# A gate table filled by scattered adding DMAs, wider units of the up matrices, and 28 down groups ahead of the up groups

## The chip, the core and the metric

The kernel runs on one core of a Trainium2 chip. The metric is the device time of one execution in microseconds (us); three runs of the kernel before took 2607.8 to 2616.74 us, median 2609.46. The engines are named as in the profile: PE is TensorE, DVE is VectorE, ACT is ScalarE, POOL is GpSimd, SP is SyncE. GpSimd issues the indirect DMAs, SyncE and ScalarE the plain ones.

## The reference

Two transformer blocks on 512 tokens of 1024 channels. The first mixes tokens (pooling and a gated delta rule) and then has a product-key expert layer; the second is gated sparse attention. The change is in the expert layer:

- Each token has 8 heads. A head scores its query halves against two tables of 128 keys, keeps the best 16 of each half, adds them in pairs (only 50 of the 256 pairs can be among the best 16), keeps the 16 best pairs, and makes gates by softmax. Pair (i1, i2) names expert 128 x i1 + i2 of 16384.
- The result is the sum over the 128 chosen experts of gate x gelu(down[e] . x) x up[e], with down and up of 16384 x 1024 float32 values.

## The kernel before, in words

Tokens 0 to 127 fetch the rows of their experts: `fetch` issues an indirect DMA on GpSimd that brings one row of 1024 values for each of 128 tokens (512 KB) into a ring buffer, and `row_step` uses it on VectorE (L1155 for the 128 down rows, L1167 for the 128 up rows, which need all down rows first). Tokens 128 to 511 (384 columns) meet all experts on TensorE, in 32 groups of 512 experts:

- `expert_down(g)`: 4 products of 24 matmuls each (8 slices of channels, three float16 terms, `mm3` at L352 to L354) and a Gelu. Groups below `R1` are computed early, and their result is stored in DRAM (`ged`); `load_gelu` brings it back.
- `load_gates(g)` brings the gates of the group's experts for all 384 tokens from the table `gd` in DRAM. `combine(g)` multiplies them with the gelu values (L1110, VectorE) and splits the product in two 16-bit parts (L1112 on ScalarE, L1113 on GpSimd).
- `expert_up(g)`: 8 products (one per 128 output channels) of 12 matmuls, each added to the residual `hT` by VectorE (L1132).

Every weight unit (1 MB, 128 x 2048 float32) goes the same way, in the order of the list `seq`: load on SP's queue into one of 4 `raw` buffers, three units ahead; squares on ScalarE (L299) for a power-of-two scale (a small chain through TensorE and VectorE); a float16 part on ScalarE (L313) and the rest on VectorE (L314), one unit ahead. Up units go to one of 2 `usp` buffers, all others to one of 3 `sp` buffers.

The table of gates is built in the gate stage. `select(tt)`, for 128 tokens, finds the best pairs with top-16 searches and turns places into expert numbers with one-hot comparisons (L1003, L1005, L1007). `gate_chunk` then makes, for 32 tokens, one-hot rows of i1 (times the gate, in two parts) and of i2 (L1048 to L1052), multiplies them on TensorE into the dense table, copies it on ScalarE (L1061) and stores it. `PLAN` is the order of selects, chunks and early down groups. After it the buffers of the gate stage are freed for the loop: down groups 12 to 31 alternate with up groups by the list `events`.

The framework's scheduler orders the instructions of each engine by priority, which follows program order, and by when it expects operands to be ready; each engine then runs its list in order. Row steps are spread by `tick(n)`: a budget starts at -6 and gains 1.6 per quarter of a fresh down group, and 1.2 or 1.0 at each second product of an up group; a row step is emitted for each whole unit. `issue_after` ties a row step behind the last residual update. What the budget has not released is emitted by `rows_done()` in front of the last up groups, which run in two parts of the tokens under the norms of the next block.

Of the kernel before, what the change touches and what calls it, by code (L numbers as in the profile page):

```python
# [20 lines left out]
P = 128  # L21
S = 512
D = 1024
# [5 lines left out]
GSC = 16384.0  # L29
PAIRS = [(a, b) for a in range(16) for b in range(16) if (a + 1) * (b + 1) <= 16]  # L30
NPAIR = len(PAIRS)
PAIR_ROWS = [(0, 1, 16), (1, 1, 8), (2, 1, 5), (3, 1, 4), (4, 1, 3), (5, 3, 2), (8, 8, 1)]
# [27 lines left out]
def shape_constants():  # L60
# [21 lines left out]
    put(c1, C1, "rcount", np.broadcast_to(1.0 / (np.arange(16)[None] + 1.0), (P, 16)))  # L82
    c2 = np.zeros((P, NC2), np.float32)
# [14 lines left out]
    c3 = np.concatenate([np.repeat(np.arange(P), 2), np.repeat(np.arange(NPAIR), 16)])  # L98
# [3 lines left out]
R1 = 12  # L102
TD = 384
RING = 6
AH = ()
PLAN = "D D s0 D D s1 g0 D g1 g2 D g3 D s2 g4 D g5 g6 D g7 D s3 g8 D g9 g10 D g11"
# [5 lines left out]
R2 = 3  # L112
# [4 lines left out]
def tile_model(ctx: ExitStack, tc: tile.TileContext, A, out, dbg=None, stop=None):  # L117
# [43 lines left out]
    # ------------------------------------------------------------------ constants  # L161
# [7 lines left out]
    c3 = cp.tile([P, 2 * P + 16 * NPAIR], F16, name="c3")  # L169
# [42 lines left out]
    # ------------------------------------------------------------------ weight stream  # L212
# [20 lines left out]
    order, fresh = [], list(range(R1, 32))  # L233
    for i in range(R1):
# [4 lines left out]
    for i in range(32):  # L239
        if i == 0:  # L240
            events += [("D", order[1]), ("D", order[2]), ("L", order[0]), ("C", order[0])]
        elif 1 < i + 1 < 32 and order[i + 1] >= R1 and i + 1 > 2:
            events.append(("D", order[i + 1]))
        if i + 2 < 32 and order[i + 2] < R1:
            events.append(("L", order[i + 2]))
        if i + 1 < 32:
            events.append(("C", order[i + 1]))
        events.append(("U", order[i]))
    for e, g in events:
        if e == "D":  # L250
            for u in range(2):
                plan(("d", g, u), A["down"][g * 2 + u], 2048, "split", group=("d", g))
        elif e == "U":
            for u in range(2):
                plan(("u", g, u), A["up"][g * 2 + u], 2048, "split", group=("u", g), usplit=g != order[31])
# [24 lines left out]
    def advance(i, loads=False, split=0):  # L280
# [38 lines left out]
        def ahead(k):  # L319
            key = seq[at[k]]["key"]  # L320
            name = "d1" if key[0] == "d" and (key[1] < R1 or key[1] in order[1:R2]) else key[0]
            p = URGENT.get(name, (0, 0))[k == "split"]
            return tc.high_priority(p) if p else ExitStack()
# [21 lines left out]
    def descale(e, isx, k=1.0):  # L345
        """1 / (scale of the weights * scale of the data), times k"""
# [25 lines left out]
    def norm_cols(nm):  # L372
        """the sums of squares of a token in its own partition, a column for each 128 tokens"""
# [12 lines left out]
    def cols_bcast(r):  # L386
        """the columns laid along the tokens, in every partition"""
# [6 lines left out]
    def weight_bound(wcol, n, nm):  # L394
        """powers of two (s, 1 / s) with s * max |w| below 2 ** 15"""
# [5 lines left out]
    def norm3_scale(wname, nm):  # L401
        """|x * rstd| <= 32: a power of two that brings x * rstd * w into range"""
# [9 lines left out]
    def norm3(nm, sl, ws, each=None, pool=False):  # L412
        """RMS norm of the tokens sl in two float16 parts"""
# [9 lines left out]
    def spread3(rows3, v):  # L423
        """rows 0..7 of v as three bfloat16 parts, 32 partitions apart"""
# [37 lines left out]
    # beta and decay rows, then their column forms  # L462
# [20 lines left out]
    def delta_gen(half, q4, k4, v4_):  # L483
# [3 lines left out]
        for n in range(NCH):  # L487
# [42 lines left out]
            # inverse of I + L, block by block  # L530
# [159 lines left out]
    # pooled branch  # L690
# [50 lines left out]
    # the delta-rule output, normalised and gated between the projections of the gates  # L741
# [71 lines left out]
    # |h2| <= 32 |gscale| + |shift| <= sqrt(2 (1024 gscale^2 + shift^2))  # L813
# [8 lines left out]
    def range_start(nm):  # L822
        """powers of two (s, 1 / s), lowered to the ranges of the products that follow"""
# [5 lines left out]
    def range_for(t, e, s, inv):  # L829
        """|sum x w| <= sqrt(sum x^2) sqrt(sum w^2), two such terms added"""  # L830
# [73 lines left out]
    # ------------------------------------------------------------------ product-key experts  # L904
    # tokens 0..127 fetch the rows of their experts, tokens 128..511 meet all experts on the tensor engine
# [13 lines left out]
    def top16(items):  # L919
        """(values, work copy, best values, their places) of several rows, step by step"""  # L920
# [38 lines left out]
    V.tensor_scalar(wk[:, 0:1], s_w, 2.0 ** -37, None, op0=ALU.mult)  # L959
    V.tensor_scalar(wk[:, 1:2], inv_w, 2.0 ** 23, None, op0=ALU.mult)  # L960
    iota_m = c3[:, 0:2 * P].rearrange("p (m e) -> p m e", e=2)
    iota_c = c3[:, 2 * P:].rearrange("p (c k) -> p c k", k=16)
    selT = s1.tile([P, 4, TD], F16, name="selT")
    i1T, i2T, ghT, glT = (selT[:, i] for i in range(4))
    gd = drp.tile([TD // 32, 2, P, 64, 32], F32, name="gdram")
    ged = drp.tile([R1, P, 4 * TD], F32, name="gedram")
    rowg = px.tile([P, P], F32, name="rowg")
    rowi = px.tile([P, 2, P], I32, name="rowi")
    rowu = px.tile([P, P], F32, name="rowu")

    def select(tt):
        sl = slice((tt - 1) * P, tt * P)
        if tt in AH:
            advance(last[0], split=2)
        idf = slab("idf")[:, 0:256].rearrange("p (f h k) -> p f h k", f=2, h=NH)
        V.tensor_copy(idf, idx[:, tt])
        V.tensor_scalar(idf[:, 0], idf[:, 0], float(P), None, op0=ALU.mult)
        cand = slab("cand")[:, :NH * NPAIR].rearrange("p (h c) -> p h c", h=NH)
        cide = slab("cide")[:, :NH * NPAIR].rearrange("p (h c) -> p h c", h=NH)
        o = 0  # L980
        for a0, na, nb in PAIR_ROWS:
            n = na * nb
            shp = [P, NH, na, nb]
            dst = lambda t: t[:, :, o:o + n].rearrange("p h (a b) -> p h a b", a=na)
            A1 = lambda t: t[:, 0, :, a0:a0 + na, None].to_broadcast(shp)
            B1 = lambda t: t[:, 1, :, None, 0:nb].to_broadcast(shp)
            V.tensor_tensor(dst(cand), A1(val[:, tt]), B1(val[:, tt]), op=ALU.add)
            G.tensor_tensor(dst(cide), A1(idf), B1(idf), op=ALU.add)
            o += n
# [3 lines left out]
        sel = tp[:, 2 * P:3 * P].rearrange("p (h k) -> p h k", h=NH)  # L993
# [3 lines left out]
        p16 = smp.tile([P, NH, 16], F16, tag="p16", name="p16", bufs=1)  # L997
        V.tensor_copy(p16, pos)
        prs = {}
        for h in range(NH + 2):  # L1000
            if h < NH:
                eq = slab("eq", (P, NPAIR, 16), F16)
                V.tensor_tensor(eq, iota_c, p16[:, h, None, :].to_broadcast([P, NPAIR, 16]), op=ALU.is_equal)  # L1003
                prs[h] = s1.tile([P, NPAIR, 16], F32, tag="eqp", name="eqp", bufs=3)
                G.tensor_tensor(prs[h], eq, cide[:, h, :, None].to_broadcast([P, NPAIR, 16]), op=ALU.mult)  # L1005
            if h >= 2:
                V.tensor_reduce(sel[:, h - 2, :], prs[h - 2].rearrange("p c k -> p k c"), AX.X, ALU.add)  # L1007
# [5 lines left out]
        if tt == 0:  # L1013
            V.tensor_tensor(rowg.rearrange("p (h k) -> p h k", h=NH), ex, sm.to_broadcast([P, NH, 16]), op=ALU.mult)
            # place of expert (u, a, p) in the rows of "up": u, p, a
            e0, e1 = rowi[:, 0], rowi[:, 1]
            V.tensor_copy(e0, tp[:, 2 * P:3 * P])
            r = smp.tile([P, 2, P], I32, tag="ei", name="ei", bufs=1)
            V.tensor_scalar(r[:, 0], e0, 127, 1, op0=ALU.bitwise_and, op1=ALU.logical_shift_left)
            V.tensor_scalar(r[:, 1], e0, 7, 1, op0=ALU.logical_shift_right, op1=ALU.bitwise_and)  # L1020
            V.tensor_scalar(e1, e0, -256, None, op0=ALU.bitwise_and)
            V.tensor_tensor(r[:, 0], r[:, 0], r[:, 1], op=ALU.bitwise_or)
            V.tensor_tensor(e1, e1, r[:, 0], op=ALU.bitwise_or)
            return
# [764 lines left out]
```

## Time and profile before

| | us |
|---|---|
| median of three runs | 2609.46 |
| span of the profiled execution (one core, so also its own time) | 2609.8 |
| TensorE busy | 2302.3 (88%) |
| VectorE busy | 2009.6 (77%) |
| ScalarE busy | 1358.3 (52%) |
| GpSimd busy | 892.5 (34%) |

Stages by the first and last instructions of their tiles: queries 678 to 787 us, gate stage 787 to 1174, loop of down and up groups 1174 to 2090, last two up groups and norms to 2137, second block to the end. In a slice row each digit is the busy share of a fortieth of the span in tenths. A line row gives instructions, busy time (overlaps counted once), the mean duration of one and the idle time before it. Matmul durations overlap, so the spacing of their starts tells the pace.

### The profile page before, as it was taken

Reading aid. Unit: us, or ns where it says so; the run is one execution under the profiler, and the core shown is the slowest. Engines: PE = TensorE matmul, PEld = TensorE weight load, DVE = VectorE, ACT = ScalarE, POOL = GpSimd, SP = SyncE. Lnnn points to the kernel's source line nnn. Section 1 sums busy time; section 2 is a strip of 40 time slices with the busy share of each in tenths; the row PEclk is TensorE's granted clock in tenths of the full one; section 3 lists DMA queues with packets and bytes.
Section 4 is the critical chain, followed back from the end, with each engine's and each line's share of the span. In section 5 each row is a group of like instructions: output and inputs, shape, how many; then the busy total and the mean of one; then the engine's idle time right before and its main releaser. Section 6 shows DMA issues by size and latency. Waiting matters only on the chain.

```text
span 2609.8 us, 37370 instructions
## 1 busy us (share of the span) xinstructions
PE 2302.3 (88%) x14242; PEld 1371.0 (53%) x14242; DVE 2009.6 (77%) x4166; ACT 1358.3 (52%) x1831; POOL 892.5 (34%) x618
## 2 busy tenths in 40 slices
PE   6999999999998766777799888898898989999997
PEld 2337896344654444444455555555554566555545
DVE  6877554396799999877898989889898973766555
ACT  6453223574545566554555555555455565454543
POOL 0002444020003645536666756665565520000000
PEclk9999999999999888889999999999999989999999
DMA  4220002343223443458788888888888724100120
GB/s 190 81 81 33 1 1 102 145 163 112 81 78 125 147 168 146 157 198 309 274 309 303 314 303 304 298 309 296 304 297 309 273 82 156 65 17 33 65 97 33
DMA packets 130771, 440.98 MB, mean 169 GB/s; under 512 B 9504, under 2 KB 61088, under 8 KB 100384
## 3 DMA queue, kind: packets, MB, share of 16 engines
q1 hardware_dynamic: 86272, 267.39, 29.1%
q0 software_dynamic: 36864, 134.23, 14.1%
q10 hardware_dynamic: 7456, 36.97, 3.5%
q8 instruction: 112, 1.84, 0.3%
q14 instruction: 67, 0.55, 0.1%
HBM read 401.86 MB, written 36.70 MB: 168 GB/s over the span
## 4 chain that ended last, share of the span: by engine, by line
PE 35%; DVE 31%; DMA 11%; issue 9%; ACT 8%; POOL 5%; SPq 0%; ACTq 0%; DVEq 0%; POOLq 0%
DVE sp L314 6%; DMA raw<-in_down_dram 4%; PE ps_in L352 4%; PE ps_in L354 4%; PE ps_in L353 4%; POOL ring L1147 3%; DMA raw<-in_up_dram 3%; DVE ohH L1052 2%; DVE rjunk L1155 2%; ACT sp L313 2%; DVE hT L1132 2%; DVE ysum L1167 2%; ACT junk L299 2%; PE ps_r L552 2%; PE ps_x L546 2%
## 5 line engine op out<-in xcount | busy, mean ns | idle before, releaser
L299 ACT ACTIVATE junk<-raw 128x2048 bf16<-128x2048 f32 (+1 forms) x202 | 383.1, 1897 | 354.5 <-DMA raw<-in_up_dram 154.7
L314 DVE SCALAR_TENSOR_TENSOR sp<-raw,scw,sp 128x2048 f16<-128x2048 f32 (+2 forms) x140 | 340.5, 2433 | 103.2 <-ACT sp L313 102.8
L352 PE MATMUL ps_u<-cexp,usp 128*128 128x384 f16 (+2 forms) x1024 | 334.9, 329 | 51.2 <-DVE hT L1132 46.9
L354 PE MATMUL ps_d<-xn,sp 128*128 128x384 f16 x1024 | 341.5, 335 | 38.7 <-DVE sp L314 38.7
L354 PEld LDWEIGHTS <-sp 128*128 128x128 f16 (+1 forms) x2320 | 230.7, 99 | 247.4 <-DVE sp L314 47.6
L352 PE MATMUL ps_d<-xn,sp 128*128 128x384 f16 x1024 | 344.2, 336 | 7.1 <-ACT sp L313 5.5
L313 ACT ACTIVATE sp<-raw,scw 128x2048 f16<-128x2048 f32 (+2 forms) x140 | 276.3, 1979 | 134.4 <-DVE scw L207 101.5
L353 PE MATMUL ps_d<-xn,sp 128*128 128x384 f16 x1024 | 343.8, 336 | 0.0
L352 PEld LDWEIGHTS <-sp 128*128 128x128 f16 (+1 forms) x2320 | 230.9, 100 | 212.2 <-issue 29.8
L353 PE MATMUL ps_u<-cexp,usp 128*128 128x384 bf16 (+2 forms) x1024 | 334.6, 328 | 1.7 <-POOL cexp L1113 1.7
L353 PEld LDWEIGHTS <-sp 128*128 128x128 f16 (+1 forms) x2320 | 230.7, 99 | 197.6 <-issue 26.5
L354 PE MATMUL ps_u<-cexp,usp 128*128 128x384 f16 (+2 forms) x1024 | 330.2, 328 | 3.7 <-DVE usp L314 3.7
L352 PE MATMUL ps_in<-xn,sp 128*128 128x512 f16 (+2 forms) x728 | 272.6, 376 | 5.8 <-DVE cv L479 3.3
L354 PE MATMUL ps_in<-xn,sp 128*128 128x512 f16 (+2 forms) x728 | 272.6, 376 | 1.5 <-DVE sp L314 1.5
L353 PE MATMUL ps_in<-xn,sp 128*128 128x512 f16 (+2 forms) x728 | 272.6, 375 | 0.0
L1147 POOL DMA_INDIRECT ring<-in_down_rows_dram,rowi x128 | 192.3, 1502 | 179.8 <-DVE rjunk L1155 109.8
L1147 POOL DMA_INDIRECT ring<-in_up_dram,rowi x128 | 190.9, 1491 | 176.1 <-DVE ysum L1167 125.9
L1113 POOL TENSOR_TENSOR cexp<-cf,cexp 128x384 bf16<-128x384 f32 x128 | 174.5, 1383 | 36.1 <-ACT cexp L1112 34.9
L1167 DVE SCALAR_TENSOR_TENSOR ysum<-ring,rowg,ysum 128x1024 f32<-128x1024 f32 x127 | 172.1, 1355 | 0.2
L1132 DVE SCALAR_TENSOR_TENSOR hT<-ps_u,yd,hT 128x384 f32<-128x384 f32 (+2 forms) x272 | 153.6, 583 | 21.5 <-PE ps_u L354 21.2
L1155 DVE SCALAR_TENSOR_TENSOR rjunk<-ring,xrow 128x1024 f32<-128x1024 f32 x128 | 164.9, 1288 | 3.1 <-DMA ring<-in_down_rows_dram,rowi 3.0
L353 PEld LDWEIGHTS <-usp 128*128 128x128 f16 x1024 | 102.1, 100 | 116.2 <-issue 58.9
(446 smaller groups left out, 4397.1 us busy)
## 6 DMA issues: line engine op xcount, KB each, us to landing
raw<-in_down_dram SPq DMA_DIRECT2D x64, 1024.0 KB, 5.5
raw<-in_up_dram SPq DMA_DIRECT2D x64, 1024.0 KB, 6.5
raw<-in_w_in_dram SPq DMA_DIRECT2D x45, 1024.0 KB, 4.8
gdram<-stg ACTq DMA_DIRECT2D x24, 1024.0 KB, 5.9
gt<-gdram SPq DMA_DIRECT2D x31, 768.0 KB, 9.0
raw<-in_w_ada_dram SPq DMA_DIRECT2D x12, 1024.0 KB, 4.8
gedram<-gelu ACTq DMA_DIRECT2D x12, 768.0 KB, 4.4
gelu<-gedram SPq DMA_DIRECT2D x12, 768.0 KB, 9.6
```

The lines of the kernel that those rows point to most:

```text
L299: act(junk[:, :e["n"]], e["raw"][:, :e["n"]], AF.Square, accum_out=ss[:, j:j + 1])
L313: act(sp[:, 0, :n], e["raw"][:, :n], AF.Copy, scale=e["s"])
L314: rq["lo"] = V.scalar_tensor_tensor(sp[:, 1, :n], e["raw"][:, :n], e["s"], sp[:, 0, :n], op0=ALU.mult, op1=ALU.subtract)
L352: T.matmul(ps, wh, xh, start=start, stop=False)
L353: T.matmul(ps, wh, xl, start=False, stop=False)
L354: T.matmul(ps, wl, xh, start=False, stop=stop)
L546: T.matmul(px[:, R4(r)], lm[:, R4(r)], Rm[:, R4(r)], start=True, stop=True)
L1113: G.tensor_tensor(ct[:, i, 1, :].bitcast(BF16), c, ct[:, i, 0, :], op=ALU.subtract)
L1132: rq["ins"] = V.scalar_tensor_tensor(o, ps[:, :n], yds[g], o, op0=ALU.mult, op1=ALU.add)
L1147: G.indirect_dma_start(out=r, out_offset=None, in_=src, in_offset=bass.IndirectOffsetOnAxis(ap=rowi[:, s // P, s % P:s % P + 1], axis=0))
L1155: V.scalar_tensor_tensor(jk, r, 1.0, xrow, op0=ALU.mult, op1=ALU.mult, accum_out=rowu[:, s:s + 1])
L1167: V.scalar_tensor_tensor(ysum[0], r, g, ysum[0], op0=ALU.mult, op1=ALU.add)
```

## The change

1. The table. `gd` becomes one array with a cell for each expert and token (expert, token; 16384 x 384 float32). 32 DMAs on SP's queue (`clear_gates`) fill it with zeros during the projections. `select` yields the gates (`gate_w`) and the cell numbers (`gate_i`, 384 x expert + token); `scatter(tt, h)` issues 16 indirect DMAs on GpSimd for head h of 128 tokens, each adding 128 values to 128 cells. Each head's DMAs wait for those of the head before it for the same tokens, the first for the clears; every `load_gates` waits for all. Place to number: no one-hot of 50 places, but comparisons with the 16 starts of the rows of pairs (float16, 16 x 16 x 8, VectorE only) and sums by halving. `gate_chunk` is gone.
2. The up matrices. A unit holds 8 expert tiles by 256 output channels instead of 2 tiles by 1024, with a scale of its own. `expert_up(q)` takes a quad of two groups: 8 products of 24 matmuls, so a residual update per 24 matmuls. `combine` takes two groups at once, one instruction of each kind per group, and the subtraction moves from GpSimd to VectorE. The rows that tokens fetch come from the natural layout (`up_rows`).
3. The order. `R1` 12 to 28: 28 down groups run in the gate stage, four in the loop. Ring of rows 6 to 4, `LAG` 4 to 3. The tick constants stay; the tick after an up product now comes after each of the 8 products of a quad.

```diff
-R1 = 12
+R1 = 28
-RING = 6
-PLAN = "D D s0 D D s1 g0 D g1 g2 D g3 D s2 g4 D g5 g6 D g7 D s3 g8 D g9 g10 D g11"
+RING = 4
+GB = 3
+PLAN = "D s1 D s2 D s3 D D D s0"
...
+    def clear_gates(g):
+        cleared.append(nc.sync.dma_start(gd.rearrange("(g p c t) o -> g p c (t o)", g=32, p=P, c=12)[g],
+                                         zero[:, None, :].to_broadcast([P, 12, P])).ins)
...
+        if 8 <= ct < 40:
+            clear_gates(ct - 8)
...
+        over_a(ge, each(p16), first_, ALU.is_ge)
+        over_a(t2, ge, step_, ALU.mult)
+        over_a(t1, ge, di, ALU.mult)
+        sum_a(st, t2)
+        sum_a(i1, t1)
...
+        over_a(ge, each(st), iota_, ALU.is_equal)
+        over_a(t2, ge, ih[:, 1], ALU.mult)
+        sum_a(i2, t2)
...
+    def scatter(tt, h):
+        key, new = f"scatter{tt}", []
+        for s in range(h * 16, h * 16 + 16):
+            i = G.indirect_dma_start(out=gd, out_offset=bass.IndirectOffsetOnAxis(ap=gate_i[tt][:, s:s + 1], axis=0),
+                                     in_=gate_w[tt][:, s:s + 1], in_offset=None, compute_op=ALU.add).ins
+            tc.declare_no_dep(i, group="scatter", keep=heads.get(tt, []), reason="other cells")
+            tc.add_to_no_dep_group("scatter", i)
+            after(i, heads.get(tt, cleared))
+            new.append(i)
+        heads[tt] = new
...
+        i = q.dma_start(gt, gd.rearrange("(g i p t) o -> g p i (t o)", g=32, i=4, p=P)[g]).ins
+        for tt in heads:
+            after(i, heads[tt])
...
+            V.scalar_tensor_tensor(t, gt, ca[:, 0:1], t, op0=ALU.mult, op1=ALU.mult)
+            nc.scalar.copy(ct[:, 0], t)
+            V.tensor_tensor(ct[:, 1].bitcast(BF16), t, ct[:, 0], op=ALU.subtract)
...
-            for i in range(4):
+            for i in range(8):
+                ct = cexp[2 * q + i // 4]
...
-            elif piece is None and dt_ % 2:
-                tick(TK[1] if g >= R1 else TK[2])
+            elif piece is None:
+                tick(TK[1] if 2 * q >= R1 else TK[2])
...
-    LAG = 4
+    LAG = 3
...
-        else:
-            gate_chunk(int(op[1:]))
+            if op != "s0":
+                for h in range(NH):
+                    scatter(int(op[1:]), h)
```

## Rows read from the trace of the kernel before

**Rows 1.** Page, slices of 65 us: TensorE, VectorE, DMA engines.
```profile
PE   6999999999998766777799888898898989999997
...
DVE  6877554396799999877898989889898973766555
...
DMA  4220002343223443458788888888888724100120
```
**Rows 2.** Windows by stage: start:end, length, busy per engine, granted clock, DMA share, GB/s.
```profile
678.00:787.00 109.00, 102.20 (x575) 58.02 (x574) 99.85 (x535) 55.68 (x70) 0.00 (x0) 0.98 0.25 88
787.00:1174.00 387.00, 277.87 (x2033) 178.70 (x2032) 344.58 (x699) 223.26 (x336) 190.29 (x108) 0.86 0.41 158
1203.00:2090.00 887.00, 786.99 (x4728) 457.62 (x4726) 797.71 (x1116) 468.93 (x490) 539.52 (x373) 0.97 0.84 297
2090.00:2137.00 47.00, 41.73 (x423) 36.45 (x424) 38.49 (x85) 27.23 (x47) 12.36 (x11) 0.93 0.20 69
2137.00:2609.00 472.00, 451.16 (x2687) 248.46 (x2685) 272.26 (x822) 236.10 (x449) 7.05 (x12) 0.98 0.19 69
```
**Rows 3.** Lines of VectorE in the gate stage, 787 to 1174 us.
```profile
L1052 DVE TENSOR_TENSOR ohH<-ohA,selT 128x1024 f16<-128x1024 f16 x48 | 93.4, 1946 | 6.1 <-PE ps_g L1057 6.1
L314 DVE SCALAR_TENSOR_TENSOR sp<-raw,scw,sp 128x2048 f16<-128x2048 f32 x24 | 63.8, 2661 | 17.8 <-ACT sp L313 17.8
...
L1048 DVE TENSOR_TENSOR ohA<-c,selT 128x1024 f16<-128x1024 f16 x48 | 37.7, 786 | 1.9 <-ACT selT L1036 1.9
...
L924 DVE FIND_INDEX8 tp<-tp,cand 128x8 uint32<-128x50 f32 x32 | 5.9, 204 | 0.0
...
L922 DVE MAX8 tp<-cand 128x8 f32<-128x50 f32 x32 | 4.0, 197 | 0.3
```
**Rows 4.** Tile ps_u: count, duration ns, first and last start.
```profile
L352 PE MATMUL ps_u<-cexp,usp x1024: 216/326/528, 1203.7 to 2133.2; 128*128 128x384 f16 x160, 128*128 128x256 f16 x6, 128*128 128x128 f16 x5
```
**Rows 5.** Waits in the loop: total us, times, longest.
```profile
ACT junk L299 <- DMA raw<-in_up_dram: 144.4, 47, 8.9
```
**Rows 6.** Timeline of TensorE at the first down group.
```profile
786.99 0.32 PE L353 MATMUL ps_d<-xn,sp 128*128 128x384 f16 x1
787.16 0.33 PE L354 MATMUL ps_d<-xn,sp 128*128 128x384 f16 x1
```
**Rows 7.** Timeline of GpSimd at the first row fetches.
```profile
1177.72 2.93 POOL L1147 DMA_INDIRECT ring<-in_down_rows_dram,rowi  x1 [0.30 <-issue]
1180.95 0.94 POOL L1147 DMA_INDIRECT ring<-in_down_rows_dram,rowi  x1 [0.30 <-issue]
1182.20 0.93 POOL L1147 DMA_INDIRECT ring<-in_down_rows_dram,rowi  x1 [0.31 <-issue]
```
**Rows 8.** Timelines of VectorE and GpSimd around 2050 us.
```profile
2050.41 2.35 DVE L314 SCALAR_TENSOR_TENSOR sp<-raw,scw,sp 128x2048 f16<-128x2048 f32 x1
...
2050.58 3.00 POOL L1147 DMA_INDIRECT ring<-in_up_dram,rowi  x1 [1.81 <-DVE dsc L348]
```
**Rows 9.** Lines of GpSimd and VectorE in the loop, 1203 to 2090 us.
```profile
L1147 POOL DMA_INDIRECT ring<-in_up_dram,rowi x128 | 190.9, 1491 | 176.1 <-DVE ysum L1167 125.9 <-DVE ssb L199 15.4 <-DVE dsc L348 7.4
...
L1167 DVE SCALAR_TENSOR_TENSOR ysum<-ring,rowg,ysum 128x1024 f32<-128x1024 f32 x127 | 172.1, 1355 | 0.2
...
L314 DVE SCALAR_TENSOR_TENSOR usp<-raw,scw,usp 128x2048 f16<-128x2048 f32 x60 | 141.8, 2379 | 5.5 <-ACT usp L313 5.4
L1132 DVE SCALAR_TENSOR_TENSOR hT<-ps_u,yd,hT 128x384 f32<-128x384 f32 x240 | 141.4, 606 | 16.4 <-PE ps_u L354 16.1
L1110 DVE SCALAR_TENSOR_TENSOR cf<-gt,cs,gelu 128x384 f32<-128x384 f32 x124 | 101.0, 831 | 23.9 <-POOL cexp L1113 18.4 <-ACT gelu L1084 5.5
```
**Rows 10.** Tile ring: time from issue to landing.
```profile
DMA to landing us min/median/max: 4.0/7.5/17.4
```
**Rows 11.** DMA in the loop: queues (packets, MB, share of 16 engines); gate loads.
```profile
q1 hardware_dynamic: 61980, 132.56, 43.6%
q0 software_dynamic: 35751, 130.15, 40.4%
...
gt<-gdram SPq DMA_DIRECT2D x30, 768.0 KB, 9.0
```

More of the change, by code (lines that the diff above doesn't have):

```diff
@@ L97, in shape_constants @@
     put(c2, C2, "qs", 0.125 / slopes[np.arange(4)[None] + 4 * (p[:, None] // 64)])
[L98 removed]
+    step = np.append(np.diff([0] + FIRST)[:15], 0)
+    c3 = np.concatenate([np.repeat(v, 8) for v in (np.array(FIRST), step, np.arange(16))])
     return c1, c2, np.broadcast_to(c3[None], (P, c3.size)).astype(np.float16)
[L102 removed]
+R1 = 28
 TD = 384
[L104 to L106 removed]
+RING = 4
+GB = 3
+PLAN = "D s1 D s2 D s3 D D D s0"
 SL3 = 40
@@ L111 @@
 URGENT = {"d1": (0, 0), "d": (50, 50), "u": (50, 50)}
-R2 = 3
 TK = (1.6, 1.2, 1.0)
@@ L232, in tile_model @@
         plan(("q", u), A["w_query"][u], 2048, "split")
-    order, fresh = [], list(range(R1, 32))
-    for i in range(R1):
+    order, fresh = [], list(range(R1 // 2, 16))
+    for i in range(R1 // 2):
         order.append(i)
@@ L238, in tile_model @@
     events = [("D", g) for g in range(R1)]
-    for i in range(32):
+    prep = lambda q: [("D" if g >= R1 else "L", g) for g in (2 * q, 2 * q + 1)]
+    pre = {i: prep(q) for i, q in enumerate(order)}
+    for i in range(16):
         if i == 0:
[L241 to L246, printed above, removed]
+            events += pre[0] + [("C", order[0])] + [e for e in pre[1] if e[0] == "D"]
+            if pre[1][0][0] == "L":
+                events += pre[1]
+        if i + 1 < 16:
             events.append(("C", order[i + 1]))
+        if i + 2 < 16 and pre[i + 2][0][0] == "L":
+            events += pre[i + 2]
         events.append(("U", order[i]))
+        if i + 2 < 16 and pre[i + 2][0][0] == "D":
+            events += pre[i + 2]
     for e, g in events:
@@ L253, in tile_model @@
         elif e == "U":
-            for u in range(2):
-                plan(("u", g, u), A["up"][g * 2 + u], 2048, "split", group=("u", g), usplit=g != order[31])
+            for u in range(4):
+                plan(("u", g, u), A["up"][g * 4 + u], 2048, "split", usplit=g != order[15] or u < 2)
     for u in range(2):
@@ L958, in tile_model, with over_a, sum_a @@
     wk = cp.tile([P, 2], F32, name="wk")
-    V.tensor_scalar(wk[:, 0:1], s_w, 2.0 ** -37, None, op0=ALU.mult)
+    V.tensor_scalar(wk[:, 0:1], s_w, 2.0 ** -23, None, op0=ALU.mult)
     V.tensor_scalar(wk[:, 1:2], inv_w, 2.0 ** 23, None, op0=ALU.mult)
[L961 to L965, printed above, removed]
+    first_, step_, iota_ = (c3[:, i * P:(i + 1) * P].rearrange("p (a h) -> p a h", h=NH) for i in range(3))
     ged = drp.tile([R1, P, 4 * TD], F32, name="gedram")
     rowg = px.tile([P, P], F32, name="rowg")
-    rowi = px.tile([P, 2, P], I32, name="rowi")
+    rowi = px.tile([P, P], I32, name="rowi")
     rowu = px.tile([P, P], F32, name="rowu")
-    def select(tt):
[L972 to L977, printed above, removed]
+    gate_w = [rowg] + [s1.tile([P, P], F32, name=f"gw{i}") for i in range(3)]
+    gate_i = [rowi] + [s1.tile([P, P], I32, name=f"gi{i}") for i in range(3)]
+    def over_a(o, a, b, op):
+        V.tensor_tensor(o, a, b[:, :, None, :].to_broadcast([P, 16, 16, NH]), op=op)
+    def sum_a(o, t):
+        n = 8
+        while n:
+            d = t[:, 0:n] if n > 1 else o
+            V.tensor_tensor(d if n > 1 else o[:, None], t[:, 0:n], t[:, n:2 * n], op=ALU.add)
+            n //= 2
+    def select(tt):
+        ih = smp.tile([P, 2, 16, NH], F16, tag="ih", name="ih", bufs=1)
+        V.tensor_copy(ih, idx[:, tt].rearrange("p f h k -> p f k h"))
+        di = smp.tile([P, 16, NH], F16, tag="di", name="di", bufs=1)
+        V.memset(di[:, 15], 0.0)
+        V.tensor_tensor(di[:, 0:15], ih[:, 0, 1:16], ih[:, 0, 0:15], op=ALU.subtract)
         cand = slab("cand")[:, :NH * NPAIR].rearrange("p (h c) -> p h c", h=NH)
-        cide = slab("cide")[:, :NH * NPAIR].rearrange("p (h c) -> p h c", h=NH)
         o = 0
@@ new lines, in select, with after @@
+        V.tensor_tensor(gate_w[tt].rearrange("p (h k) -> p h k", h=NH), ex, sm.to_broadcast([P, NH, 16]), op=ALU.mult)
+        if tt:
+            V.tensor_scalar(gate_i[tt], ef, float(TD), k1("pidx")[:, tt - 1:tt], op0=ALU.mult, op1=ALU.add)
+            return
+        V.tensor_copy(rowi, ef)
+    def after(i, names):
+        for n in names:
+            tc.add_manual_dep(i, n.name, mybir.DependencyInfo(mybir.DependencyClass.Sync, mybir.DependencyReason.DATA),
+                              reason="table of gates")
@@ new lines, in tile_model @@
+    heads = {}
+    def scatter(tt, h):
[8 more added lines that the diff above has]
+        heads[tt] = new
@@ L1070, in expert_down @@
     def expert_down(g):
-        t = px.tile([P, 4, TD], F32, tag="gelu", name="gelu", bufs=3)
+        t = px.tile([P, 4, TD], F32, tag="gelu", name="gelu", bufs=GB)
         gs = None
@@ L1092, in load_gelu @@
     def load_gelu(g):
-        t = px.tile([P, 4, TD], F32, tag="gelu", name="gelu", bufs=3)
+        t = px.tile([P, 4, TD], F32, tag="gelu", name="gelu", bufs=GB)
         nc.sync.dma_start(t.rearrange("p i t -> p (i t)"), ged[g])
@@ L1210, in tile_model @@
     pools["s"] = None
-    nU = 0
-    load_gates(order[0], nc.scalar)
+    nU, lg = 0, [g for q in order for g in (2 * q, 2 * q + 1)]
+    for g in lg[:2]:
+        load_gates(g, nc.scalar)
     for e_, g in ev:
@@ L1218, in tile_model @@
         elif e_ == "C":
-            combine(g)
-            if nU + 2 < 32:
-                load_gates(order[nU + (1 if g == order[0] else 2)])
+            combine(2 * g, 2 * g + 1)
+            nU += 2
+            for x in lg[nU:nU + 2]:
+                load_gates(x)
         elif e_ == "U":
-            if nU < 30:
+            if g != order[15]:
                 expert_up(g)
-            nU += 1
     rows_done()
```

144 lines of the change are left out of this document (44 added, 100 removed).

## The prediction

> **What bounds the kernel now.** I read the page's slices first [rows 1], then the windows by stage [rows 2]: the projections up to 787 us keep TensorE busy and the change leaves their products alone; so does block 2 from 2137 us on (472 us, TensorE busy 451). Between lie two stretches that the change rebuilds. In the gate stage (787 to 1174) VectorE is busy 345 of 387 us and TensorE 278 at a granted clock of 0.86: it is bound by VectorE, which builds one-hot tables (L1052 alone 93 us [rows 3]). In the loop of down and up groups (the first up product starts at 1203.7 [rows 4]; to 2090) three resources are near full together: VectorE 798 of 887 us, TensorE 787, DMA 0.84. The squares of the weight units wait 144 us for their loads [rows 5], so DMA is felt too.
>
> At full clock products of 384 columns start 0.163 us apart [rows 6]: a group, up or down, has 96 of them, 15.6 us. 64 groups are 1000 us of the 1350 between 787 and 2137.
>
> **Down groups early.** 28 instead of 12 run in the gate stage. TensorE needs 28 x 15.6 = 437 us; with block 2's share (451/472) 16.4 us a group. VectorE is the limit first: four selects, each with top-16 searches (40 instructions on 50 elements plus their value loads; the busy times of such a row are 4.0 to 5.9 us for 32 [rows 3], with the loads 8 us a select), five passes over 2048 float16 elements, three trees of 1920, and short ones. A 1024-element pass cost 0.79 us at L1048, 1.95 at L1052 beside GpSimd tensor work, which is now gone. So 2048 elements lie between 1.3 and 3.9; I take 1.3, as L1048, and 27 us a select (bounds 23 to 40), 30 with what is left of the query stage. A down group costs VectorE two L314 (2.66 each) and some short ones, 6.2 us. Six groups lie in the stretch of the selects: 4 x 30 + 6 x 6.2 = 157 us, to 944. The other 22 take 22 x 16.4 = 361: TensorE is out of down groups at **1305**. One fresh group (16 us) can follow; the second fresh one needs a gelu buffer that combine frees.
>
> **The scatter.** The removed matmuls, ACT copies and one-hot passes go, and with them 24 stores. In their place GpSimd issues 3 x 8 x 16 = 384 indirect DMAs of 128 four-byte cells. The trace has no scatter; the nearest row is the indirect row fetch, also 128 descriptors. Back to back and undisturbed it takes 0.94 us with 0.31 us between, 1.25 a DMA; beside VectorE's L314 it takes 2.9 to 3.0 [rows 7, 8], and its mean in the loop is 1.49 [rows 9], so 1.80 with the gap. L314 fills 26% of the loop and 5.3/16.4 = 32% of the down groups, so 1.80 is my price while these run, 1.25 when VectorE is idle. Each head of 16 waits on GpSimd for the 16 before it on the same tokens; behind that wait stand all later scatters and the row fetches. A landing takes 4.0 us at least, 7.5 at the median [rows 10]; I take 4.0 per 16, 0.25 a DMA (bounds 0, if other tokens' heads fill in, and 0.47). The adding itself: nothing to a further 0.94 us a DMA, if the read of the old cell counts as a second set of descriptors; I take nothing, as the row fetch.
>
> The first select ends at about 787 + 48 = 835 (one down group's splits, the rest of the queries, itself). Until 1305: 470 / (1.80 + 0.25) = 229 DMAs. The other 155 at 1.25 + 0.25 = 1.50: 233 us. The scatter ends at **1538**. No gates can be loaded before, since every table row gets cells from every token. Gates then land in 9.0 us [rows 11], combine needs about 6 (1.9 multiply, 2.0 cast, 1.9 subtract, by L1110 and L1167 scaled to 1536 elements): first up product at 1553, **+349 us** on 1203.7. TensorE stands idle from about 1321.
>
> The Trainium skill's SBUF page ("SBUF — State Buffer", section "Who interferes with whom") would have it milder: a VectorE instruction with two SBUF inputs takes only the shared read interface, and writing descriptors, by inference there, needs the write interface. L314 has two SBUF inputs, and [rows 8] show a fetch stretched to 3.00 us beside it, so I go by the row; by the page alone the price under the down groups would be 1.25, which would give the time of the second rival.
>
> **The loop.** It keeps 30 up groups, 3 down groups and, by the tick budget, 142 row steps in place of 256. (Ticks: -6 to start, 4 x 4 x 1.6 for fresh down groups, 13 quads x 8 x 1.0 and 2 x 8 x 1.2 for up: 142.8. Before, 20 fresh down groups gave 128 alone, and the sum was 257.) VectorE per up group: two usp splits 4.8, four hT updates instead of eight 2.4, four row steps 5.3, multiply and subtract of two halves of a quad's gates (the subtract comes over from GpSimd) 3.7, ten small ones 1.8: 18.0 us; per down group 14.9. That is 585 us. The same prices give 880 for the loop before, where 798 were busy, so 530, and at the share of before (0.90) 590. TensorE: 33 x 15.65 = 516, at its 0.89 580. DMA: rows at 0.404 x 887 us for 130.15 MB, 248 rows of 512 KB, 1.45 us each [rows 11], 206; 118 MB of weights, gates and gelu at 342 GB/s, 346; 552, at its 0.84 657. I take the mean, **609 us instead of 887, -278** (580 to 660; the upper end also holds the two usp buffers, each now freed every 7.8 us against 4.4 us of splitting, which can wait behind row steps).
>
> **The tail.** 114 rows are left for the flush in front of the last quad, all of them up rows, with four ring buffers: a buffer's round is landing 4.0, wake-up 0.7 and a row step of 1.3 us, so 1.5 us a row at least, 2.4 at the median landing, 1.44 by DMA alone. I take 1.65: 188 us. The last quad's products hide beside them, but the norms need tokens 0 to 127: some 38 us more to block 2. Before, 47 us [rows 2]. **+179 us.**
>
> **At nothing.** The 32 clears (25 MB) lie in the projections, where the DMA slices read 0 to 4 [rows 1]; without that cover each delays a load by 768 KB / 342 GB/s = 2.3 us, 74 in all; range only. More scale chains for the up units are in the 18.0 us.
>
> **Sum.** 349 - 278 + 179 = +250. The profiled span is 2609.8 us, the median of the runs 2609.46: no offset. Forecast **2860 us**.
>
> **Rivals.**
> 1. The adds cost GpSimd a second set of descriptors: 2.74 + 0.25 under the down groups, 2.19 + 0.25 after: 157 DMAs by 1305, 227 x 2.44 = 554, end 1859, 321 later: **3181**. For it: nothing here has ever added. Against: the instruction is the fetch's.
> 2. L314 holds the scatter up less than it does a fetch: 470 / 1.50 = 313 by 1305, 71 x 1.50, end 1412: **2734**; with head waits hidden too, about 2637. For it: fetches beside the f32 row steps stay at 0.94 often. Against: 2.9 and 3.0 us beside L314. The SBUF page of the Trainium skill speaks for it.
> 3. Faster: the scatter finishes under the down groups. It decides at (1305 - 835) / 384 = 1.22 us a DMA, all in. Then TensorE sets the first product at 1321 + 15 = 1336, +132; with the loop at its lower end (580, -307) and rows at the pace of DMA (114 x 1.44 + 38 - 47 = +155): -20, **2590**. For it: a fetch alone is at 1.25. Against: every wait must vanish.
>
> **Numbers.** Forecast 0.50, first rival 0.20, second 0.24, third 0.06. The range leaves out the third and a piece of the second at the bottom, and the worse half of the first at the top: 2640 to 3100. Slower by over 0.3% (about what a measurement of this kernel can tell from no change) 0.92, within 0.02, faster 0.06.
>
> **What would show it.** 384 indirect DMAs on GpSimd from about 835 us, near 2.0 us apart until 1305, near 1.5 after; TensorE idle for some 230 us in front of the first up product, with its granted clock down; the hT updates halved; a stretch of 114 row steps with nothing on TensorE after the last quad. Wrong if the gap in front of the up groups is under 100 us (then 2 or 3), if adds stand far apart with VectorE idle (then 1), or if the row steps at the end are few.

## The result, and the profile after

The changed kernel takes 3166.47 us (median of three runs, 3162.16 to 3172.52) against 2609.46: 1.213 times as long, 95% interval 1.210 to 1.216. The forecast was 2860, its range ended at 3100. Slower was right; the size was not.

The slices of the page after (79 us each, in the order TensorE, VectorE, ScalarE, GpSimd, granted clock, DMA):

```profile
PE   6999999999899200000099988898888004999997
...
DVE  6885545769963000000033578887888666476545
ACT  6552245654666000000066735554554002555543
POOL 0023431000488888887710133333334664000000
PEclk9999999999999655555599999999999556999999
DMA  9810024422466322222265688878987883410121
```

The hole in the middle is expected in kind, not in size: TensorE, VectorE and ScalarE have six empty slices each, five of them in common, in which only GpSimd works. A second hole, of two slices on TensorE and ScalarE, lies ahead of block 2. The windows by stage (start:end, length, busy time of TensorE, weight loads, VectorE, ScalarE, GpSimd, granted clock, DMA share, GB/s) answer to [rows 2]:

```profile
827.00:1050.00 223.00, 208.82 (x1272) 123.80 (x1273) 129.16 (x422) 134.30 (x138) 186.00 (x103) 0.97 0.64 174
1050.00:1584.00 534.00, 0.00 (x0) 0.00 (x0) 0.00 (x0) 0.00 (x0) 436.35 (x282) 0.50 0.21 0
1584.00:1822.00 238.00, 236.52 (x1471) 142.19 (x1471) 105.40 (x177) 157.30 (x160) 14.31 (x10) 0.99 0.63 225
1822.00:2420.00 598.00, 528.67 (x3159) 309.14 (x3158) 495.78 (x819) 297.41 (x230) 215.52 (x137) 0.97 0.84 301
2420.00:2690.00 270.00, 53.98 (x457) 43.97 (x454) 180.56 (x194) 34.15 (x54) 150.56 (x123) 0.59 0.70 238
2690.00:3160.00 470.00, 445.20 (x2652) 245.32 (x2652) 266.35 (x811) 231.35 (x440) 5.51 (x9) 0.98 0.19 65
```

The second row is the surprise: for 534 us no engine but GpSimd executes anything. The third is the second surprise: behind the hole TensorE runs for 238 us without a break, and still not on up products. They are the down groups 16 to 28, which were to lie beside the scatter, and the first two fresh ones. The tiles say the same: the first up product [rows 4] moved from 1203.7 to 1821.9 us, the scatter ran from 826.7 to its last start at 1581.3, the next block's first product of its tile `ps_nat` starts at 2676.1 (before: 2127.5).

```profile
L357 PE MATMUL ps_u<-cexp,usp x1024: 217/326/528, 1821.9 to 2674.5; 128*128 128x384 f16 x160, 128*128 128x128 f16 x6, 128*128 128x256 f16 x5
...
L1059 POOL DMA_INDIRECT gdram<-gw,gi x384: 1546/1547/4572, 826.7 to 1581.3; - x192
...
L1304 PE MATMUL ps_nat<-sp,xn x32: 336/336/548, 2676.1 to 2708.7; 128*128 128x408 f16 x32
```

TensorE's waits (in all, times, the longest) give the two holes a name each:

```profile
PE ps_d L357 <- ACT gelu L1085: 540.2, 3, 537.6
PE ps_yt L1191 <- DVE ysum L1170: 186.9, 1, 186.9
```

The first is not a wait for gates. A down product waits for a Gelu to free its PSUM buffer; so ScalarE is what stands still. The timeline of its restart (start, duration, engine, line) shows for what:

```profile
1584.42 0.38 ACTq L1100 DMA_DIRECT2D gt<-gdram  x1
1584.85 0.58 ACT L1085 ACTIVATE gelu<-ps_d,dsc 128x384 f32<-128x384 f32 x1 [546.20 <-DMA gdram<-gw,gi]
1585.04 0.37 ACTq L1100 DMA_DIRECT2D gt<-gdram  x1
...
1585.48 0.48 PE L357 MATMUL ps_d<-xn,sp 128*128 128x384 f16 x1 [537.62 <-ACT gelu L1085]
```

The first two loads of gates are issued from ScalarE's list (`load_gates(g, nc.scalar)`), and each waits for all 384 scatters. In the list the first stands just behind the store of the 14th of the 28 early down groups, and all Gelus of the other fourteen but one stand behind it. ScalarE sat 546 us at that DMA, from 1038.6; by 1047.9 TensorE had ended group 15, three products beyond the last Gelu, and stopped. ScalarE's splits stand in the same list, VectorE's wait for those (548.5 us at the longest), and the weight loads moved nothing from then on. The Trainium skill's page "PSUM — Partial Sum Buffer" (section "Engine vs sequencer instructions") calls ScalarE's queue strict FIFO; the trace agrees, with 546.20 us on one row. In program order those loads come after all early groups; the scheduler placed them by when it took the table to be ready, and that it took the scatter to be far shorter is inferred from where they stand.

### The profile page after: what moved, and what is told of

It is laid out like the page before. It is cut to its first block, busy times and chain, and to the rows that moved or that the text cites. A ratio compares the mean times of both kernels' runs of the same rounds, so it can differ in the third digit from the quotient of the medians.

```text
span 3160.4 us, 35429 instructions
## 1 busy us (share of the span) xinstructions
PE 2234.4 (71%) x13465; PEld 1324.4 (42%) x13465; DVE 1750.5 (55%) x4018; ACT 1260.0 (40%) x1534; POOL 1137.3 (36%) x766
## 3 DMA queue, kind: packets, MB, share of 16 engines
q8 instruction: 105, 1.72, 0.2%
## 4 chain that ended last, share of the span: by engine, by line
PE 33%; POOL 20%; DVE 16%; DMA 14%; issue 10%; ACT 6%; SPq 0%; POOLq 0%; ACTq 0%; DVEq 0%
POOL gdram L1059 18%; DMA raw<-in_up_dram 4%; DMA ring<-in_up_rows_dram,rowi 4%; DVE usp L319 3%; PE ps_in L357 3%; PE ps_in L359 3%; PE ps_in L358 3%; DVE sp L319 3%; PE ps_d L357 2%; PE ps_d L358 2%; PE ps_d L359 2%; ACT sp L318 2%; ACT junk L304 1%; DVE rjunk L1158 1%; PE ps_r L569 1%
## 5 line engine op out<-in xcount | busy, mean ns | idle before, releaser
L1059 POOL DMA_INDIRECT gdram<-gw,gi x384 | 622.7, 1622 | 402.4 <-PE ps_ss L204 268.8
L319 DVE SCALAR_TENSOR_TENSOR sp<-raw,scw,sp 128x2048 f16<-128x2048 f32 (+2 forms) x140 | 327.5, 2340 | 728.7 <-ACT sp L318 728.7
L357 PE MATMUL ps_d<-xn,sp 128*128 128x384 f16 x1024 | 336.6, 329 | 544.2 <-ACT gelu L1085 540.2
L1150 POOL DMA_INDIRECT ring<-in_down_rows_dram,rowi x128 | 202.7, 1584 | 557.5 <-DVE rjunk L1158 368.9
L359 PE MATMUL ps_u<-cexp,usp 128*128 128x384 f16 (+2 forms) x1024 | 336.3, 329 | 7.3 <-DVE usp L319 7.2
L359 PE MATMUL ps_d<-xn,sp 128*128 128x384 f16 x1024 | 335.6, 328 | 5.6 <-DVE sp L319 5.6
L357 PE MATMUL ps_u<-cexp,usp 128*128 128x384 f16 (+2 forms) x1024 | 336.7, 330 | 0.0
L358 PE MATMUL ps_d<-xn,sp 128*128 128x384 f16 x1024 | 336.4, 329 | 0.0
L1085 ACT ACTIVATE gelu<-ps_d,dsc 128x384 f32<-128x384 f32 x128 | 73.0, 575 | 653.8 <-DMA gdram<-gw,gi 546.2
L1150 POOL DMA_INDIRECT ring<-in_up_rows_dram,rowi x128 | 166.5, 1300 | 131.0 <-DVE ysum L1170 57.7
L1170 DVE SCALAR_TENSOR_TENSOR ysum<-ring,rowg,ysum 128x1024 f32<-128x1024 f32 x127 | 163.1, 1284 | 70.7 <-DMA ring<-in_up_rows_dram,rowi 69.3
L318 ACT ACTIVATE usp<-raw,scw 128x2048 f16<-128x2048 f32 x62 | 124.1, 2001 | 162.5 <-PE ps_u L359 159.3
```

The source lines that it names most:

```text
L318: act(sp[:, 0, :n], e["raw"][:, :n], AF.Copy, scale=e["s"])
L319: rq["lo"] = V.scalar_tensor_tensor(sp[:, 1, :n], e["raw"][:, :n], e["s"], sp[:, 0, :n], op0=ALU.mult, op1=ALU.subtract)
L357: T.matmul(ps, wh, xh, start=start, stop=False)
L358: T.matmul(ps, wh, xl, start=False, stop=False)
L359: T.matmul(ps, wl, xh, start=False, stop=stop)
L1059: i = G.indirect_dma_start(out=gd, out_offset=bass.IndirectOffsetOnAxis(ap=gate_i[tt][:, s:s + 1], axis=0), in_=gate_w[tt][:, s:s + 1], in ...
```

## Experiments

Each ratio is to the kernel before on the same chip. e1 to e3 and e5 ran beside a median of 2607.9 us, e4 and e6 to e8 beside 2604.9, e9 beside 2605.9.

**e1: the gate loads behind the last early Gelu.**

```diff
-            act(t[:, i, :], ps[:, :TD], AF.Gelu, scale=gs)
+            rq["gelu"] = act(t[:, i, :], ps[:, :TD], AF.Gelu, scale=gs)
...
-    for g in lg[:2]:
-        load_gates(g, nc.scalar)
+    with tc.issue_after(rq["gelu"].ins):
+        for g in lg[:2]:
+            load_gates(g, nc.scalar)
```

> Only edit: the first two gate loads are issued on ScalarE behind the last early Gelu instead of behind the fourteenth down group. Theory A (the gate load in ScalarE's list waits for the scatter and holds back the Gelus of 14 down groups): these run under the scatter, TensorE is out of down groups near 1290 us, the first up product comes near 1605 instead of 1822, time about 2950 us. With the scatter slowed beside the down groups by VectorE (2.17 instead of 1.85 us a DMA, as from 827 to 1050) it ends some 35 us later: 2985. Rival (the down groups stop because something else is missing, buffers or loads that the scatter delays): they stop at the same place, no change, 3166.

Measured: 2973.61 us, ratio 1.140 (1.136 to 1.143), 193 us less than the change and near theory A (2950 to 2985). All early groups now run beside the scatter and the first up product starts at 1633.4 (1821.9 before the mending). The longest waits of TensorE and VectorE in e1:

```profile
PE ps_d L357 <- ACT gelu L1085: 346.8, 3, 344.5
DVE gelu L1112 <- DMA gt<-gdram: 356.7, 3, 350.5
```

TensorE is out of early down groups at 1248 and stops at 1260 in group 29, whose Gelus stand behind the moved loads. The scatter itself is not touched (last start 1591.9), and the hole left, 345 us, is its own: `combine` (L1112) waits for the gates. Behind the scatter's end TensorE first runs the rest of group 29 and group 30, 120 matmuls in all, and then the first up product. So the place of these loads on ScalarE costs 193 of the 557 us.

**e2: the scatter without its adding**, on top of e1 (each DMA overwrites its cells, the addition is left out).

```diff
-                                     in_=gate_w[tt][:, s:s + 1], in_offset=None, compute_op=ALU.add).ins
+                                     in_=gate_w[tt][:, s:s + 1], in_offset=None).ins
```

> As the run with the gate loads behind the down groups, and the 384 scattered DMAs write instead of adding (a cell that two heads hit keeps one value). Theory B (adding costs GpSimd a second set of descriptors): a DMA takes 0.94 us again, 1.25 with the gap, the scatter ends near 1340, the first up product near 1360, 245 us earlier than in that run: about 2705. Rival (four-byte cells scattered into DRAM cost the 1.55 us, whatever the operation): as that run, about 2950.

Measured: 2795.25 us, 1.072 (1.069 to 1.075). GpSimd's timeline with nothing beside it, first the change, then e2:

```profile
1299.99 1.55 POOL L1059 DMA_INDIRECT gdram<-gw,gi  x1 [0.30 <-issue]
1301.84 1.55 POOL L1059 DMA_INDIRECT gdram<-gw,gi  x1 [0.30 <-issue]
```
```profile
1330.14 0.96 POOL L1059 DMA_INDIRECT gdram<-gw,gi  x1 [0.30 <-issue]
1331.41 0.96 POOL L1059 DMA_INDIRECT gdram<-gw,gi  x1 [0.30 <-issue]
```

Adding costs GpSimd 0.59 us a DMA; a plain scatter costs what a fetch does (0.94 [rows 7]). The time is nearer to theory B than to the rival; it falls short of B because the scatter still ran to 1414 (first up product at 1453.6): beside the down groups a plain DMA is held up too. From 1050 to 1250 us, down groups alone beside it, 128 DMAs started in e2, 1.56 us each, and 102 in e1, 1.96. Counted over the whole scatter, the DMAs that overlap a split on VectorE (L319), and no other of its instructions, by over 0.3 us took 1.72 us on average in e2 (95 of them) and 1.79 in e1 (91), those that overlap none so long 0.96 and 1.55. Beside a split the adding thus costs next to nothing more; the two prices do not add up.

**e3: the row steps spread over the shorter loop.**

```diff
-TK = (1.6, 1.2, 1.0)
+TK = (2.8, 1.9, 1.8)
```

> Only edit: tick constants 2.8, 1.9, 1.8 instead of 1.6, 1.2, 1.0, so that the budget releases all 256 rows in the loop and none is left for the flush. Theory C (the rows are bound by DMA and VectorE, so they are only moved): the loop grows from 598 to about 760 us (114 rows at 1.45 us of DMA), the tail shrinks from 270 to about 60, time about 3120. Rival (they fit into the loop's idle time): 3166 - 200 = 2960. Other rival (the loop is slowed more than that, since DMA would have to move 500 GB/s at TensorE's pace): no gain, 3166 or more.

Measured: 3069.54 us, 1.176 (1.172 to 1.179), 97 us less than the change, between theory C (3120) and its rival (2960). The second hole is gone; `ysum` is done at 2545 instead of 2646, and block 2 starts at 2581.0:

```profile
L1170 DVE SCALAR_TENSOR_TENSOR ysum<-ring,rowg,ysum x127: 1267/1275/1285, 2176.7 to 2544.1; 128x1024 f32<-128x1024 f32 x127
```

So of the 225 us that the flush takes (2420 to 2645) 97 come back; by most of the rest the loop grows when the rows stand in it (719 us from the first up product to the last row, where the loop without them took 598).

**e5: twelve early groups, scatter and quads as they are.**

```diff
-R1 = 28
+R1 = 12
```

> Only edit: 12 early down groups instead of 28, the rest as changed; the tick budget then releases all rows again. The gate load stands behind the twelfth down group with nothing but the loop behind it. Theory A: nothing is held back that could run, the first up product comes near 1600; the loop takes about 887 us as before the change, the tail 47: about 3010. Rival (28 early groups are worth their time even so, since 16 more groups in the loop cost 16 x 17 us and TensorE idles before): 3100 to 3170.

Measured: 3020.22 us, 1.156 (1.152 to 1.160), as theory A had it (3010). The first up product starts at 1601.5, right behind the scatter, since all twelve groups were done before ScalarE came to its wait; TensorE waits for the gates themselves:

```profile
PE ps_u L357 <- ACT cexp L1113: 571.7, 1, 571.7
```

As ordered, the 28 early groups made the kernel 146 us slower than twelve would have. That includes the flush: with twelve the budget releases all rows in the loop, which alone was worth 97 us in e3.

**e6: e1 and e3 together.**

> Both mendings together: the gate loads behind the last early Gelu (2973.6 us alone) and the row steps spread over the whole loop (TK 2.8, 1.9, 1.8; 97 us gained alone). Theory A (two separate losses, one before the first up product and one behind the last): 2973.6 - 97 = 2877 us, with the first up product still near 1633. Rival (the row steps had room only because the loop ran late; in the earlier loop they hold it up): 2930 or more. Either way above 2800: with the adding scatter ending near 1590 the up groups cannot start early enough to come near the kernel before.

Measured: 2889.79 us, 1.109 (1.107 to 1.112); the first up product at 1632.6, block 2 at 2396.4. 84 us less than e1, against 97 when spread alone: two separate losses, within 13 us, as theory A had it (2877). What is left is 285 us; e7 tries the scatter for it.

**e7: e1 with a third of the scatter** (the gates of tokens 256 to 511 are left out of the table).

```diff
-            if op != "s0":
+            if op == "s1":
```

> The gate loads behind the last early Gelu, and only the scatter of tokens 128 to 255 (128 of 384 indirect DMAs); the gates of tokens 256 to 511 are left out. Theory A (GpSimd's time in the 384 adding DMAs sets the first up product): the scatter ends by 1110, the down groups at about 1300, the first up product at about 1320 instead of 1633, and the time is 2973.6 - 313 = 2660 us. Rival (something else is late as well: the table's loads, the down groups' weights): the first product stays past 1450 and the time above 2790.

Measured: 2618.05 us, 1.0055 (1.0035 to 1.0075); theory A had 2660. The up products and the scatter in e7:

```profile
L357 PE MATMUL ps_u<-cexp,usp x1024: 217/326/528, 1279.8 to 2132.1; 128*128 128x384 f16 x160, 128*128 128x128 f16 x6, 128*128 128x256 f16 x5
...
L1059 POOL DMA_INDIRECT gdram<-gw,gi x128: 1546/1547/4572, 823.9 to 1117.1; - x128
```

With the scatter over at 1119 the down groups set the first up product: 1279.8 (the prediction's third rival had 1336 for that case). GpSimd's time in the 384 DMAs is thus what the up groups wait for in e1, and nothing else stood behind it: first product and time both fall by some 355 us. With the scatter hidden the kernel is still no faster than before; it has the flush.

**e4: the quads alone**, with the gate table, the `PLAN` and the twelve early groups of before (the ring of four rows and `LAG` 3 stay as changed): the kernel after with `gate_chunk`, `select` and `load_gates` put back, and

```diff
-R1 = 28
+R1 = 12
...
-            V.scalar_tensor_tensor(t, gt, ca[:, 0:1], t, op0=ALU.mult, op1=ALU.mult)
+            for i in range(4):
+                ti = t[:, i, :].rearrange("p (c t) -> p c t", t=32)
+                V.scalar_tensor_tensor(ti, gt[:, :, i, :], ca[:, 0:1], ti, op0=ALU.mult, op1=ALU.mult)
```

> The up matrices in units of eight expert tiles by 256 columns alone: gate table by one-hot products, twelve early down groups and the selects as before, row steps spread as before. Theory A (the quads are no gain and no loss: the weight stream and the row steps set the loop; with twelve early groups the loop and the row steps behind it took 945 us in e5 against 934 before): first up product near 1204, 2610 to 2640 us. Rival (halved updates of hT and wider copies and subtractions free VectorE and ScalarE, and the loop shortens): 2540 us or less.

Measured: 2619.59 us, 1.0066 (1.0037 to 1.0094): no gain, a small loss, as theory A had it. First up product 1211.4, block 2 at 2134.0: 922.6 us between, before 923.8. VectorE was busy 758 us of that against 826 before; the loop did not shorten for it. TensorE's waits from 1270 to 2090 us, in the kernel before and then in e4, show where the gain went:

```profile
PE ps_u L352 <- DVE hT L1132: 45.2, 20, 5.9
PE ps_ss L203 <- DVE ssb L199: 19.7, 16, 2.9
```
```profile
PE ps_ss L204 <- DVE ssb L200: 72.7, 30, 6.7
```

The waits for the update of `hT` are gone, and the waits for the scale chains of the weight units (`ps_ss`) have grown by 53 us. ScalarE, which squares the units and splits them, waited 97.5 us for a free `usp` buffer in that stretch, before 25.4; that its squares come late for that reason is likely, and was not tried.

**e8: quads, one-hot table, twenty early groups.** e4 with

```diff
-R1 = 12
-PLAN = "D D s0 D D s1 g0 D g1 g2 D g3 D s2 g4 D g5 g6 D g7 D s3 g8 D g9 g10 D g11"
-TK = (1.6, 1.2, 1.0)
+R1 = 20
+PLAN = "D D s0 D D s1 D g0 D g1 D g2 D g3 D s2 D g4 D g5 D g6 D g7 D s3 D g8 D g9 D g10 D g11"
+TK = (2.0, 1.4, 1.3)
```

> As e4, with twenty early down groups instead of twelve, the eight more put between the chunks of the gate table where TensorE has gaps, and row steps spread over the loop (TK 2.0, 1.4, 1.3). Theory A (the gate stage is bound by VectorE, so the eight groups of 15.6 us of TensorE lie mostly beside it, and each group taken out of the loop gives back 6 to 12 us as from e5 to e3): 2540 to 2600 us, the fastest of all here. Rival (their Gelus and splits hold up the chunks by all their 125 us): 2650 us or more.

Measured: 2587.48 us, ratio 0.9940 (0.9915 to 0.9965): the only version that beats the kernel before.

**e9: the same without the quads**, that is the kernel before with these three lines, and with

```diff
-            events += [("D", order[1]), ("D", order[2]), ("L", order[0]), ("C", order[0])]
+            events += [("D", x) for x in order[1:3] if x >= R1] + [("L", order[0]), ("C", order[0])]
```

> The kernel before (one-hot gate table, up matrices in pairs) with only the twenty early down groups, the place of the eight more among the chunks and the row steps' spread of e8. Theory A (e8's gain comes from these alone, and the quads cost what e4 cost against the kernel before, 2619.6 to 2604.9): 2587.5 - 14.7 = 2573 us, ratio 0.988. Rival (the early groups pay only because the quads halve the updates of hT in a loop that TensorE then bounds): 2600 us or more, ratio 0.998 or above.

Measured: 2627.21 us, 1.0082 (1.0055 to 1.0109): slower. Theory A falls; by the time the rival holds. Lines of the products and updates of the loop in e8, then in e9 (count, busy time, mean ns, idle time before and what ended it):

```profile
L357 PE MATMUL ps_u<-cexp,usp 128*128 128x384 f16 (+2 forms) x1024 | 341.4, 334 | 0.0
...
L1131 DVE SCALAR_TENSOR_TENSOR hT<-ps_u,yd,hT 128x384 f32<-128x384 f32 (+2 forms) x132 | 78.7, 597 | 15.2 <-PE ps_u L359 10.4 <-PE ps_ss L204 4.7
```
```profile
L352 PE MATMUL ps_u<-cexp,usp 128*128 128x384 f16 (+2 forms) x1024 | 342.9, 336 | 40.1 <-DVE hT L1132 27.4
...
L1132 DVE SCALAR_TENSOR_TENSOR hT<-ps_u,yd,hT 128x384 f32<-128x384 f32 x240 | 142.4, 606 | 22.5 <-PE ps_u L354 22.2
```

Both pay about 60 us in the gate stage for the eight groups: the first up product starts at 1272.3 in e8 (1211.4 in e4) and at 1262.1 in e9 (1203.7 before). From there to block 2 (2103.5 and 2142.1) the quads get 922.6 - 831.2 = 91 us back, the pairs 923.8 - 880.0 = 44. Where the pairs wait for the update of `hT` (27.4 us at L352) the quads do not wait. But they wait longer for the scale chains; from 1270 to 2090 us, e8 and then e9:

```profile
PE ps_ss L204 <- DVE ssb L200: 115.5, 43, 11.2
```
```profile
PE ps_ss L203 <- DVE ssb L199: 55.5, 23, 6.4
```

In all TensorE is idle for 127 us between its first up product and block 2 in e8 and for 147 in e9: 20 of the 49 us by which the two stretches differ. The other 29 are TensorE's busy time; one more fresh down group lies behind the first up product in e9 (eleven, in e8 ten). Quads alone gain nothing, early groups alone lose; together they gain 0.6%. The rival's reason, the update of `hT`, is not proven: the trace gives it less than 30 us of waits, against 60 us more for the scale chains. The quads also moved the subtraction of `combine` to VectorE and widened it, e8 has its own order of events and a ring of four rows, and none of that was taken apart.

## Why the prediction was wrong, by its steps

The change took 550.6 us more by the spans (3160.4 and 2609.8), where +250 was forecast. By terms: first up product +618 for +349; loop 886 to 598, -288 for -278; from the loop's end to `ps_nat` 38 to 256, +219 for +179; block 2 +2. The misses are 269, -10, 40 and 2.

- **The step that failed** is "TensorE is out of down groups at 1305": it had done 15 of the 28 by 1048 and stood until 1585. The prediction put every load of gates behind the scatter, rightly, and then did not ask on which engine the waiting load stands and what is queued behind it. e1 prices the step: 188 us of the first product, 193 of the time. Without it the kernel takes 2974 us, which lies inside the range. Of the 269 us missed, 81 are left.
- **The scatter** was near in sum under the down groups, by two errors that cancel. The adding, taken at nothing, costs 0.59 us alone (e2); the hold by the split, taken at 1.80 us a DMA with its gap and 2.05 with the head waits, was dearer than it is, as rival 2 had it (1.50 all in; a plain DMA took 1.56). So in e1 204 DMAs had started by 1248, 2.08 us each. That the errors came out even is luck. Behind the down groups nothing cancels: the other 180 took 345 us, head waits included, 1.92 each, where 1.50 was forecast, +75. TensorE was out of the early groups at 1248 instead of 1305, which at the forecast's prices would have ended the scatter at 1518 instead of 1538, -20; and from the scatter's end to the first product it took 40 us instead of 15, +25, since one and a quarter down groups came first. These are the 81, within 1. The first rival asked for 2.19 us plus head waits with VectorE idle; 1.55 + 0.30 lies between it and the forecast. Rival 3's point, 1.22 us all in, is below even a plain scatter with nothing beside it, 0.96 + 0.30.
- **Head waits** at 0.25 us a DMA: 20 us in eleven waits over the whole scatter of the changed kernel, 0.05 a DMA. Cheaper than taken.
- **Selects, early groups and clears**: the scatter began at 826.7, forecast 835. In e1 the six down groups beside the selects took 114 us (790 to 904), forecast 157, and the other 22 took 15.65 each, forecast 16.4. The clears moved 25 MB in the first 135 us or so (the page reads 300 and 267 GB/s in the first two slices), and the first down product came at 793.2 instead of 786.8: 6 us at most, taken at nothing.
- **The loop**, 598 for 609: right, though the forecast was the mean of three bounds (590, 580 and 657) and so in part by luck. VectorE was busy 496 us where 530 were reckoned, TensorE 529 for 516, and the DMA share was 0.84 as taken. The updates halved as said, 120 of 609 ns for 240 of 606, with 122 + 14 row steps among them. The lines of the changed kernel's loop:

```profile
L1158 DVE SCALAR_TENSOR_TENSOR rjunk<-ring,xrow 128x1024 f32<-128x1024 f32 x122 | 148.2, 1215 | 7.8 <-DMA ring<-in_down_rows_dram,rowi 7.8
...
L1135 DVE SCALAR_TENSOR_TENSOR hT<-ps_u,yd,hT 128x384 f32<-128x384 f32 x120 | 73.1, 609 | 18.2 <-PE ps_u L359 18.1
...
L1170 DVE SCALAR_TENSOR_TENSOR ysum<-ring,rowg,ysum 128x1024 f32<-128x1024 f32 x14 | 17.8, 1275 | 0.0
```

- **The flush**: 114 row steps, as counted, but 2.0 us each, not 1.65 (first start 2419.4, last 2644.8). In the flush VectorE waits in 72 of 109 steps for the row, 67.7 us:

```profile
L1170 DVE SCALAR_TENSOR_TENSOR ysum<-ring,rowg,ysum x109: 1275/1284/1350, 2424.2 to 2638.4; 128x1024 f32<-128x1024 f32 x109
...
  DVE ysum L1170: 67.7, 72
```

  109 x 1.284 + 67.7 = 208 of the 214 us. The wake-ups in a buffer's round, taken at 0.7 us, stood on no row; the runs show 0.27 from a row step's end to the next fetch (the changed kernel) and 0.09 from a landing to the step that waited for it (e4). A round of four rows at 2.0 us leaves some 6.3 us for the landing (an estimate: 8.0 - 1.28 - 0.36; the trace has no landing in the flush), between the minimum and the median of [rows 10], where the prediction took a value near the minimum. Whether six buffers would do better was not tried.
- **The contention rule.** The prediction weighed the Trainium skill's "SBUF — State Buffer" ("Who interferes with whom"), by whose inference a VectorE instruction with two SBUF inputs does not hold up the writing of descriptors. The row was the better guide: plain scatters took 1.72 us beside L319, which has two such inputs, and 0.96 alone (e2).

Could the scatter version have won with everything mended? In e6 it is at 2890. 384 x 1.85 = 710 us from 827 put the table's end at 1537 even undisturbed, 333 later than the up groups began before, and the loop gave back 288; the flush comes on top. What was worth having in the change is the quads with more early groups (e8).

## What to carry to other kernels

A DMA that waits stands in the list of the engine that issues it, and everything later in that list waits with it. When a change makes a producer slow, look up who issues each of its readers, and move the waiting issue to an engine with nothing behind it, or tie it behind the work that must not wait. An edit that takes away one wait gains nothing alone where another wait ends at the same time (e4: 45 us of waits for `hT` gone, 53 more for the scale chains); it can still decide whether another edit pays (e8 against e9), so the two are to be tried together.

## What the runs showed of the hardware that was not expected

- An indirect DMA of 128 four-byte cells took GpSimd 0.96 us when it wrote and 1.55 when it added, with 0.30 between, nothing beside it. Beside a split of VectorE (L319) it took 1.72 and 1.79.
- Adding also occupies the DMA engines. In idle stretches of the change (1100 to 1500 us, 213 DMAs) and of e2 (1300 to 1400, 74 DMAs), packets, MB and share of 16 engines:

```profile
q0 software_dynamic: 30528, 0.12, 21.3%
```
```profile
q0 software_dynamic: 2336, 0.04, 1.8%
```

  That is 0.213 x 400 x 16 / 213 = 6.4 us of one engine for a DMA that adds, in 143 packets, and 0.018 x 100 x 16 / 74 = 0.39 us for one that writes, in 32.
- In the hole TensorE's granted clock was 0.50, the level of 1.2 GHz, after standing idle, and its matmuls started 0.32 us apart at the restart instead of 0.163; but the 238 us behind it average 0.99. The clock cost little; the hole itself was the loss.
